# The last product of a decoder layer: four PSUM tiles, groups of two, one and one, and a half row in two pieces

## The chip, the cores and the metric

The kernel runs on one core of one Trainium2 chip. The core has TensorE (PE in the profile, its weight loads PEld), VectorE (DVE), ScalarE (ACT), GpSimd (POOL) and SyncE (SP, which here only starts transfers). Tiles live in SBUF; matmuls write into PSUM, which has banks of 512 f32 columns on each of 128 partitions. The metric is the device time of one execution in microseconds, as the median of several runs. The profile is one execution more, with a time of its own.

## The reference

One layer of a hybrid decoder on 1024 tokens of width 1024, in float32: a combined input projection, four heads of differential attention and four of mLSTM, an output projection with a residual, and a gated MLP (width 2816, with a causal convolution of width 3) with a residual and a final RMSNorm. What matters here are the last lines:

```python
    hn = rmsnorm(x, ffn_norm_w[l])
    u = causal_dwconv(hn @ w_up[l], ffn_conv_w[l], ffn_conv_b[l])
    gate, up = jnp.split(u, 2, axis=-1)
    x = x + (jax.nn.silu(gate) * up) @ w_down[l]
return rmsnorm(x, final_norm_w)
```

where `rmsnorm(x, w)` is `x * rsqrt(mean(x*x) + 1e-6) * w`, taken over a token's row of 1024.

## The kernel before

A product in float32 is made of three matmuls of a split operand (high and low part, `mm3b`, lines 162 to 165). The down projection, 1024 x 2816 by 2816 x 1024, is done by a fast scheme of seven products in place of eight: `PORDER = (1, 2, 7, 5, 6, 4, 3)`. Each product has 11 steps along the inner dimension (`NP`), and in each step four token tiles of 128 rows (`tt` from 0 to 3) get three matmuls of 128x512 each, 12 per step. The sums are gathered in eight rows of tiles `x2[0..7]` (128 tokens x 1024), each of which already holds the residual. `x2[4..7]` are complete one product before the end; `x2[0..3]` get their last half row (columns 512 to 1024) from the last product, number 3.

`banks(n)` gives product n its four PSUM regions: for an even n two tiles `big` of 1024 columns (two banks each, two token tiles in each), for an odd n four tiles of 512 columns, two of the tag `mm` and one each of `sa` and `sb`. The products before it, those of the up projection, take `mm`, `big` and the small ones in turn; the last of them writes an `mm` tile, and its result is added on DVE in line 1030.

`dprep_to` prepares the operands of coming steps (splits in line 115 on ACT and 116 on DVE), four steps ahead. `evac` puts the additions of a finished token tile into the list `later`, `work(n)` issues n of them; an addition is line 1202 on DVE (`add`), which reads PSUM and SBUF.

The final RMSNorm is spread out. `half` (line 1227) squares half a row on ACT and sums it through the accumulator, in two instructions; `half1` does it for the half row that is complete earlier, and multiplies it with the norm's weights `fin`. `finish(tts, h)` does the rest for the token tiles `tts`: it turns the sum of the first half into `v` (line 1242), squares the second half, adds its sum (line 1245), takes the reciprocal root on DVE (for several tiles `rsqrt`, lines 75 to 81, and line 1250; for one tile `newton`, lines 878 to 882), scales one half row on ACT (line 1254) and the other on DVE (line 1255), and starts the transfer to `out` from SP's queue (line 1260; for tile 3 in two halves, from ACT's and SP's queues, lines 1257 and 1258).

The last product keeps back its last five steps (`TAIL = 5`): after step 6 they are done token tile by token tile, 15 matmuls each, in the groups of `LAST`:

```python
LAST = ([0, 1, 2], [3])
```

After each group come its additions and its `finish`. The order of instructions on each engine is not written out: a planner orders them by the place in the code and by when it holds them ready, and an instruction of a later line may be put ahead of one that waits. Waits between engines are put in by the same framework.

Of the kernel before, what the change touches and what calls it, by code (L numbers as in the profile page):

```python
# [10 lines left out]
F32 = mybir.dt.float32  # L11
F32R = mybir.dt.float32r
I32 = mybir.dt.int32
AF = mybir.ActivationFunctionType
ALU = mybir.AluOpType
PSUM = bass.MemoryType.PSUM

P = 128
S = 1024
D = 1024  # L20
NT = S // P
# [8 lines left out]
SLOPE = [2.0 ** (-8.0 * (h + 1) / H) for h in range(H)]  # L30
LEAD = 5
DLEAD = 4
LAST = ([0, 1, 2], [3])
HELD = 4
YB = 3
RSC = -2.0 ** -13
# [3 lines left out]
def tile_hybrid(ctx: ExitStack, tc: tile.TileContext, I: dict, out: bass.AP):  # L40
    nc = tc.nc
    V = nc.vector
    A = nc.scalar
# [3 lines left out]
    cp = ctx.enter_context(tc.tile_pool(name="cp", bufs=1))  # L47
# [21 lines left out]
    def sm8(n=8, name="s8"):  # L69
        return sp.tile([P, n], F32, name=name, tag=name)  # L70

    def rsqrt(v, n, k=""):

        y = sm8(n, "rs_a" + k)
        V.tensor_scalar(y.bitcast(I32), v.bitcast(I32), -0.5, 1597463007.0, op0=ALU.mult, op1=ALU.add)
        for i in range(3):
            u = sm8(n, "rs_u" + k)
            V.tensor_tensor(u, y, y, op=ALU.mult)
            V.scalar_tensor_tensor(u, u, -0.5, v, op0=ALU.mult, op1=ALU.mult)
            y2 = sm8(n, f"rs_{i}" + k)  # L80
            V.scalar_tensor_tensor(y2, u, 1.5, y, op0=ALU.add, op1=ALU.mult)
            y = y2
        return y
# [28 lines left out]
    def split(dst, src, loeng, scale=None):  # L112

        if scale is None:
            A.activation(dst[:, 0, :], src, AF.Copy)  # L115
            loeng.tensor_tensor(dst[:, 1, :], src, dst[:, 0, :].bitcast(F32), op=ALU.subtract)  # L116
        else:
            A.activation(dst[:, 0, :], src, AF.Copy, scale=scale)
            V.scalar_tensor_tensor(dst[:, 1, :], src, scale, dst[:, 0, :].bitcast(F32), op0=ALU.mult, op1=ALU.subtract)
# [55 lines left out]
    def small(shape):  # L175

        flip[0] ^= 1
        return psA.t(shape, tag="sa" if flip[0] else "sb")

    def big(shape):  # L180
        return psA.t(shape, tag="big", bufs=2)

    def mmps():
        return psA.t([P, 512], tag="mm", bufs=2)

    def rotate(n):
        return (mmps, lambda: big([P, 512]), lambda: small([P, 512]))[n % 3]()

    def banks(n):
        if n % 2 == 0:  # L190
            b = [big([P, S]) for _ in range(2)]
            return [b[k // 2][:, HV[k % 2]] for k in range(4)]
        return [mmps(), mmps(), small([P, 512]), small([P, 512])]
# [6 lines left out]
    def load_x(i, hf, between=None):  # L200
        f = pa.t(XS, tag="ta", bufs=4)
        for c in ([slice(0, 1), slice(1, 2)] if between else [slice(0, 2)]):
            nc.sync.dma_start(f[:, c, :], I["xT"][:, 2 * i + c.start:2 * i + c.stop, HV[hf]])
            if between and c.start == 0:
                between()
        return f
# [45 lines left out]
    f = load_x(0, 0, lambda: next(g0))  # L252
    next(g0)
    split_x(0, 0, f)
    f = load_x(1, 0)
# [5 lines left out]
    f = load_x(2, 0)  # L261
# [3 lines left out]
    f = load_x(3, 0)  # L265
# [5 lines left out]
    for i in range(4):  # L271
        f = load_x(i, 1)
# [115 lines left out]
    for ct in range(4, 8):  # L388
        for hf in range(2):
            ps = rotate(2 * ct + hf)  # L390
# [406 lines left out]
    x2 = []  # L797
# [78 lines left out]
    def newton(v):  # L876
        y = sm8(1, "rx_0")
        V.tensor_scalar(y.bitcast(I32), v.bitcast(I32), -0.5, 1597463007.0, op0=ALU.mult, op1=ALU.add)
        for i, c in enumerate((3.0, 12.0, 768.0)):
            u, y2 = sm8(1, "rx_u"), sm8(1, f"rx_{i + 1}")  # L880
            V.scalar_tensor_tensor(u, y, v, y, op0=ALU.mult, op1=ALU.mult)
            V.scalar_tensor_tensor(y2, u, -c, y, op0=ALU.add, op1=ALU.mult)
            y = y2
        return y
# [239 lines left out]
    def weights(p, i):  # L1124
        if i % 2 == 0:
            wload(p, i)
        return wb.pop((p, i))
# [28 lines left out]
    def dprep_to(n):  # L1156
        while dp_[0] < min(n, len(steps)):
            p, i = steps[dp_[0]]
            if p in SUMS:
                dst, x_, y, op = SUMS[p]  # L1160
                V.tensor_tensor(blk[dst, i], blk[x_, i], blk[y, i], op=op)
            last = p == PORDER[-1] and i >= NP - 2
            if last and not ext:
                e = pd.t([P, 8, 512], F32R, "a21")
                ext.extend(e[:, 2 * m:2 * m + 2, :] for m in range(4))
            at = (lambda: w2.pop(0) if w2 else pd.t([P, 2, 512], F32R, "w2", 2)) if dp_[0] % 5 == 4 else wtile
            dops[dp_[0]] = [ext.pop(0) if last else at() for _ in range(2)]
            for dst, src in zip(dops[dp_[0]], (blk[OPS[p][0], i], weights(p, i))):
                split(dst, src, V)
            dp_[0] += 1  # L1170

    pd = None
# [15 lines left out]
    pd = Scope("pd")  # L1188
# [3 lines left out]
    x2 = [pd.t([P, D], tag="x2", bufs=8) for _ in range(NT)]  # L1192
    fin = pd.t([P, D], tag="fin")
    acc = {(p, tt): pd.t([P, 512], tag=f"acc{p}", bufs=4) for p in (1, 7) for tt in range(4)}

    def dmm(ps, k, tt, first, last):
        s_, m_ = dops[k]
        t = slice(tt * P, (tt + 1) * P)
        mm3b(ps, s_[:, 0, t], s_[:, 1, t], m_, first, last)

    def add(dst, x, y=None):
        V.tensor_tensor(dst, dst if y is None else x, x if y is None else y, op=ALU.add)  # L1202

    later = []

    def work(n):

        for _ in range(min(n, len(later))):
            later.pop(0)()

    def evac(p, tt, ps):

        h0, h1 = HV
        c11, c12, c21, c22 = x2[tt][:, h0], x2[tt][:, h1], x2[tt + 4][:, h0], x2[tt + 4][:, h1]
        if p in (1, 7):
            A.activation(acc[p, tt], ps, AF.Copy)
        if p == 6:
            a1, a7 = acc[1, tt], acc[7, tt]
            pairs = [(a1, ps), (a7, a1), (c22, a7), (c21, a7), (c12, a1)]
        else:  # L1220
            pairs = [(dst, ps) for dst in {1: [c11], 2: [c11], 5: [c12, c22], 4: [c21], 3: [c12]}.get(p, ())]
        later.extend(lambda d=d, x=x: add(d, x) for d, x in pairs)

    def half(tt, h, part):

        j = pd.t([P, 512], tag="junk")
        A.activation(j, x2[tt][:, HV[h]], AF.Square, accum_out=part)

    part1, part2 = cp.tile([P, NT], F32, name="part1"), cp.tile([P, NT], F32, name="part2")

    def half1(tt, h):

# [1 line left out]
        xx = x2[tt][:, HV[h]]  # L1234
        V.tensor_tensor(xx, xx, fin[:, HV[h]], op=ALU.mult)

    def finish(tts, h):

        n = len(tts)
        c = slice(tts[0], tts[0] + n)  # L1240
        v = sm8(n, f"vx{n}")
        V.tensor_scalar(v, part1[:, c], 1.0 / D, EPS, op0=ALU.mult, op1=ALU.add)
        for tt in tts:
            half(tt, h, part2[:, tt:tt + 1])
        V.scalar_tensor_tensor(v, part2[:, c], 1.0 / D, v, op0=ALU.mult, op1=ALU.add)
        if n == 1:
            r = newton(v)
        else:
            r = rsqrt(v, n, "x")
            V.tensor_scalar(r, r, 1.0 / RSC, None, op0=ALU.mult)  # L1250
        a_, b_ = HV[1 - h], HV[h]
        for i, tt in enumerate(tts):
            xx, ri = x2[tt], r[:, i:i + 1]
            A.activation(xx[:, a_], xx[:, a_], AF.Copy, scale=ri)
            V.scalar_tensor_tensor(xx[:, b_], xx[:, b_], ri, fin[:, b_], op0=ALU.mult, op1=ALU.mult)
            if tt == 3:
                A.dma_start(out[tt, :, a_], xx[:, a_])
                nc.sync.dma_start(out[tt, :, b_], xx[:, b_])
            else:
                nc.sync.dma_start(out[tt], xx)  # L1260

    k = 0
    TAIL = 5
    for n, p in enumerate(PORDER):
        ps = banks(n)
        last = n == len(PORDER) - 1
        for i in range(NP - TAIL if last else NP):
            dprep_to(k + 1 + DLEAD)
            fill(k)
            work(3)  # L1270
            for tt in range(4):
                dmm(ps[tt], k, tt, i == 0, i == NP - 1)
            k += 1
        if not last:
            for tt in range(4):
                evac(p, tt, ps[tt])
            if p == 2:
                later.extend(lambda tt=tt: half1(tt, 0) for tt in range(4))
            elif p == 6:
                later.extend(lambda tt=tt: half1(tt, 1) for tt in range(4, NT))  # L1280
            elif p == 4:
                later.append(lambda: finish(range(4, NT), 0))
        else:
            dprep_to(len(steps))
            for tts in LAST:
                for tt in tts:
                    for i in range(TAIL):
                        dmm(ps[tt], k + i, tt, False, i == TAIL - 1)
                    evac(p, tt, ps[tt])
                work(len(later))  # L1290
                finish(tts, 1)
    psA.close()
    pd.close()
    wp.close()
# [63 lines left out]
```

## Time and profile before

| | |
|---|---|
| median of 3 runs | 1214.32 us (1213.82 to 1214.63) |
| the profiled execution | 1213.26 us, span of its instructions 1211.5 us |
| granted TensorE clock, mean | 0.995 |
| busy: PE, DVE, ACT, POOL | 98%, 74%, 47%, 40% |
| first matmul of the first down product | 991.5 us |
| last matmul | 1201.8 us |
| last instruction that starts a transfer | 1207.7 us |

The span goes from the first instruction to the end of the last; the time of an execution is some 2 us longer. A row of the timeline gives the start, the duration, the engine, the line, the operation, what is written and what is read, and in brackets how long the engine stood idle before it and what ended that. Rows that end in "x2" or "x3" merge neighbours: start of the first, end of the last less that start.

### The profile page before, as it was taken

What the parts mean: (1) busy time and instruction counts of PE and PEld (TensorE: products, weight loads), DVE (VectorE), ACT (ScalarE), POOL (GpSimd) and SP (SyncE); (2) the same over time, 40 slices, a digit from 0 to 9 for tenths busy, and PEclk for the clock granted to TensorE, in tenths of its full rate; (3) what the DMA queues carried; (4) which work ended last, traced back from release to release, by engine and by line L of the source; (5) the groups of instructions that cost most, each with busy time, mean ns of one, the idle gap of its engine ahead of it and who ended that gap; (6) DMA issues with size and microseconds to landing.
All of it is one profiled execution on the core that took longest, in us unless ns stands there. A gap on an engine that the chain in (4) does not pass through costs nothing.

```text
span 1211.5 us, 15939 instructions
## 1 busy us (share of the span) xinstructions
PE 1183.0 (98%) x5622; PEld 973.3 (80%) x5622; DVE 899.2 (74%) x1564; ACT 571.0 (47%) x1114; POOL 480.1 (40%) x364
## 2 busy tenths in 40 slices
PE   9998999999999999999999999999999999999996
PEld 7885788888778878888888888888888888888885
DVE  5598232566767777669998998788887878886694
ACT  6534323334666666344644444434344345544462
POOL 0475451003543431001198887888887600000000
PEclk9998999999999999999999999999999999999999
DMA  8755664124212243332322312222222169823223
GB/s 307 252 206 205 226 243 166 62 71 157 79 52 54 70 157 114 121 127 99 124 70 87 103 72 100 91 70 87 77 80 104 54 217 346 296 96 96 96 79 139
DMA packets 61743, 159.03 MB, mean 131 GB/s; under 512 B 6176, under 2 KB 10464, under 8 KB 61664
## 3 DMA queue, kind: packets, MB, share of 16 engines
q1 hardware_dynamic: 61232, 157.21, 38.0%
q8 instruction: 44, 0.72, 0.3%
q10 hardware_dynamic: 432, 0.82, 0.2%
q14 instruction: 35, 0.29, 0.1%
HBM read 116.02 MB, written 37.78 MB: 127 GB/s over the span
## 4 chain that ended last, share of the span: by engine, by line
PE 84%; DVE 5%; DMA 3%; ACT 3%; POOL 3%; issue 1%; SPq 1%; POOLq 0%; ACTq 0%; DVEq 0%
PE mm L160 6%; PE mm L158 6%; PE mm L159 6%; PE mm L163 5%; PE mm L164 5%; PE mm L165 5%; PE big L158 4%; PE big L160 4%; PE big L159 4%; PE big L164 4%; PE big L165 4%; PE big L163 4%; PE sb L777 3%; POOL vda L327 3%; PE sb L158 2%; PE sb L160 2%
## 5 line engine op out<-in xcount | busy, mean ns | idle before, releaser
L115 ACT ACTIVATE w<-wf 128x512 fp32r<-128x512 f32 x160 | 97.7, 624 | 142.3 <-POOL wf L999 33.6
L116 DVE TENSOR_TENSOR w<-wf,w 128x512 fp32r<-128x512 f32 x128 | 108.4, 858 | 27.9 <-ACT w L115 21.7
L1041 DVE SCALAR_TENSOR_TENSOR y<-x2b,fcw,y 128x1022 f32<-128x1022 f32 x44 | 91.8, 2125 | 0.0
L1040 DVE SCALAR_TENSOR_TENSOR y<-x2b,fcw,y 128x1023 f32<-128x1023 f32 x44 | 75.7, 1762 | 9.4 <-ACT y L1039 9.4
L116 POOL TENSOR_TENSOR w<-s,w 128x512 fp32r<-128x512 f32 x40 | 69.8, 1746 | 6.2 <-ACT w L115 6.2
L327 POOL TENSOR_TENSOR vda<-vda 128x512 f32<-128x512 f32 x24 | 46.6, 1958 | 63.7 <-DMA vda<-in_w_down_dram 62.9
L116 POOL TENSOR_TENSOR w<-wf,w 128x512 fp32r<-128x512 f32 x32 | 46.9, 1469 | 57.0 <-ACT w L115 47.2
L116 POOL TENSOR_TENSOR w<-wu,w 128x512 fp32r<-128x512 f32 x40 | 66.5, 1662 | 1.8 <-ACT w L115 1.8
L158 PE MATMUL mm<-xb,w 128*128 128x512 f32 x168 | 66.1, 394 | 0.0
L160 PE MATMUL mm<-xb,w 128*128 128x512 f32 x168 | 65.9, 392 | 0.0
L159 PE MATMUL mm<-xb,w 128*128 128x512 f32 x168 | 65.9, 392 | 0.0
L968 POOL TENSOR_TENSOR s<-wu 128x512 f32<-128x512 f32 x20 | 36.5, 1825 | 58.0 <-DMA wu<-in_w_up_dram 58.0
L752 DVE CUSTOM_DVE_ANT_0 s<-big,B 128x128 f32<-128x128 f32 (+7 forms) x64 | 47.6, 755 | 13.7 <-PE big L750 12.3
L1039 ACT ACTIVATE y<-x2b,fcw 128x1024 f32<-128x1024 f32 x44 | 52.3, 1237 | 9.6 <-DVE x2b L1030 8.4
L754 ACT ACTIVATE s<-s,mb 128x128 f32<-128x128 f32 (+7 forms) x64 | 49.3, 772 | 11.2 <-DVE mb L753 10.0
L163 PE MATMUL big<-w 128*128 128x512 f32 x132 | 51.5, 390 | 0.8 <-DVE x L1202 0.8
L164 PE MATMUL big<-w 128*128 128x512 f32 x132 | 51.4, 389 | 0.0
L165 PE MATMUL big<-w 128*128 128x512 f32 x132 | 51.3, 389 | 0.0
L115 ACT ACTIVATE w<-wu 128x512 fp32r<-128x512 f32 x48 | 29.7, 625 | 40.1 <-PE mm L160 10.7
L777 PEld LDWEIGHTS sb<-vda,aT 128*128 128x128 f32 x288 | 36.2, 190 | 15.4 <-ACT aT L774 14.6
L777 PE MATMUL sb<-vda,aT 128*128 128x128 f32 x288 | 44.2, 289 | 3.7 <-ACT aT L774 3.1
L115 ACT ACTIVATE w<-hb 128x512 fp32r<-128x512 f32 x41 | 25.8, 630 | 44.9 <-PE big L165 19.8
(514 smaller groups left out, 3769.8 us busy)
## 6 DMA issues: line engine op xcount, KB each, us to landing
wf<-in_w_up_dram SPq DMA_DIRECT2D x22, 512.0 KB, 4.5
actd<-y SPq DMA_DIRECT2D x21, 512.0 KB, 2.6
wu<-in_w_up_dram SPq DMA_DIRECT2D x20, 512.0 KB, 3.4
wf<-in_w_st_dram SPq DMA_DIRECT2D x12, 512.0 KB, 4.2
vda<-in_w_down_dram SPq DMA_DIRECT2D x12, 512.0 KB, 6.6
wsum<-vda SPq DMA_DIRECT2D x12, 512.0 KB, 3.0
wf<-in_w_mv_dram SPq DMA_DIRECT2D x12, 512.0 KB, 5.3
wf<-wsum SPq DMA_DIRECT2D x12, 512.0 KB, 3.4
```

The costliest lines, as they stand in the source:

```text
L115: A.activation(dst[:, 0, :], src, AF.Copy)
L116: loeng.tensor_tensor(dst[:, 1, :], src, dst[:, 0, :].bitcast(F32), op=ALU.subtract)
L158: PE.matmul(ps, sh, mh, start=first, stop=False)
L159: PE.matmul(ps, sh, ml, start=False, stop=False)
L160: PE.matmul(ps, sl, mh, start=False, stop=last)
L163: PE.matmul(ps, sh, w[:, 0, :], start=first, stop=False)
L164: PE.matmul(ps, sl, w[:, 0, :], start=False, stop=False)
L165: PE.matmul(ps, sh, w[:, 1, :], start=False, stop=last)
L327: GP.tensor_tensor(dst, x_, y, op=ALU.subtract)
L777: PE.matmul(ops, aT[:, b * P:(b + 1) * P], vda[k // 2][:, k % 2, h * P:(h + 1) * P], start=k == 0, stop=k == qt)
L1040: V.scalar_tensor_tensor(y[:, 1:], u[:, :S - 1], cw[:, 1:2], y[:, 1:], op0=ALU.mult, op1=ALU.add)
L1041: V.scalar_tensor_tensor(y[:, 2:], u[:, :S - 2], cw[:, 0:1], y[:, 2:], op0=ALU.mult, op1=ALU.add)
```

## The change

The last product gets four PSUM tiles of its own, because `banks` is now called with n + 1, which flips the tags of all seven products: numbers 0, 2, 4 and 6 in order take `mm`, `mm` and the two small ones, numbers 1, 3 and 5 the two `big` ones. The groups become [0, 1], [2] and [3]. `finish` no longer scales: it returns a function `scale` that does, which is called at once for [0, 1] and for the earlier rows. For [2] it is kept, and called within `finish` of [3], behind the square of the first piece. For tile 3 the last half row is added and squared in two pieces of 256 columns (`QS`), each with an accumulator of its own (`part1` and `part2` have one more column for that) and a sum of its own on DVE. The numbers of matmuls, scalings and transfers stay as they were; one addition, one square with its accumulator read, and one small sum on DVE are added in all.

```diff
-LAST = ([0, 1, 2], [3])
+LAST = ([0, 1], [2], [3])
...
-    part1, part2 = cp.tile([P, NT], F32, name="part1"), cp.tile([P, NT], F32, name="part2")
+    part1, part2 = (cp.tile([P, NT + 1], F32, name=f"part{i}") for i in (1, 2))
+    QS = (slice(512, 768), slice(768, 1024))
...
-    def finish(tts, h):
+    def finish(tts, h, between=None):
...
         V.tensor_scalar(v, part1[:, c], 1.0 / D, EPS, op0=ALU.mult, op1=ALU.add)
-        for tt in tts:
-            half(tt, h, part2[:, tt:tt + 1])
-        V.scalar_tensor_tensor(v, part2[:, c], 1.0 / D, v, op0=ALU.mult, op1=ALU.add)
+        if tts[0] == 3:
+            for i, q in enumerate(QS):
+                j = pd.t([P, 512], tag="junk")
+                pt = part2[:, 3 + 5 * i:4 + 5 * i]
+                A.activation(j[:, 0:256], x2[3][:, q], AF.Square, accum_out=pt)
+                if i == 0:
+                    between()
+                V.scalar_tensor_tensor(v, pt, 1.0 / D, v, op0=ALU.mult, op1=ALU.add)
+        else:
+            for tt in tts:
+                half(tt, h, part2[:, tt:tt + 1])
+            V.scalar_tensor_tensor(v, part2[:, c], 1.0 / D, v, op0=ALU.mult, op1=ALU.add)
...
-        for i, tt in enumerate(tts):
-            xx, ri = x2[tt], r[:, i:i + 1]
-            A.activation(xx[:, a_], xx[:, a_], AF.Copy, scale=ri)
...
+        def scale():
+            for i, tt in enumerate(tts):
+                xx, ri = x2[tt], r[:, i:i + 1]
+                A.activation(xx[:, a_], xx[:, a_], AF.Copy, scale=ri)
+                V.scalar_tensor_tensor(xx[:, b_], xx[:, b_], ri, fin[:, b_], op0=ALU.mult, op1=ALU.mult)
+                if tt == 3:
+                    A.dma_start(out[tt, :, a_], xx[:, a_])
+                    nc.sync.dma_start(out[tt, :, b_], xx[:, b_])
+                else:
+                    nc.sync.dma_start(out[tt], xx)
+
+        return scale
...
-        ps = banks(n)
+        ps = banks(n + 1)
...
-                later.append(lambda: finish(range(4, NT), 0))
+                later.append(lambda: finish(range(4, NT), 0)())
...
+            scale = None
             for tts in LAST:
                 for tt in tts:
                     for i in range(TAIL):
                         dmm(ps[tt], k + i, tt, False, i == TAIL - 1)
-                    evac(p, tt, ps[tt])
+                    if tt < 3:
+                        evac(p, tt, ps[tt])
+                    else:
+                        for q in QS:
+                            add(x2[3][:, q], ps[3][:, q.start - 512:q.stop - 512])
                 work(len(later))
-                finish(tts, 1)
+                if tts == [2]:
+                    scale = finish(tts, 1)
+                else:
+                    finish(tts, 1, scale)()
```

More of the change, by code (lines that the diff above doesn't have):

```diff
@@ L1251, in finish @@
         a_, b_ = HV[1 - h], HV[h]
-        for i, tt in enumerate(tts):
-            xx, ri = x2[tt], r[:, i:i + 1]
[L1254 to L1260, printed above, removed]
+        def scale():
[9 more added lines that the diff above has]
+        return scale
     k = 0
```

## The prediction

> **What bounds the kernel now.** I read the page's busy shares and the shares of its chain first, then a table of busy time by stretch over the last two hundred microseconds, then the timeline of the last twenty, engine by engine.
>
> ```profile
> span 1211.5 us, 15939 instructions
> PE 1183.0 (98%) x5622; PEld 973.3 (80%) x5622; DVE 899.2 (74%) x1564; ACT 571.0 (47%) x1114; POOL 480.1 (40%) x364
> PE 84%; DVE 5%; DMA 3%; ACT 3%; POOL 3%; issue 1%; SPq 1%; POOLq 0%; ACTq 0%; DVEq 0%
> ...
> 1051.00:1081.00 30.00, 30.00 (x134) 24.86 (x133) 29.77 (x50) 16.28 (x32) 0.00 (x0) 1.00 0.31 102
> 1171.00:1187.00 16.00, 16.00 (x72) 13.24 (x71) 13.59 (x32) 10.98 (x23) 0.00 (x0) 1.00 0.39 148
> ...
> 1187.00:1190.50 3.50, 3.50 (x17) 2.90 (x16) 0.00 (x0) 0.00 (x0) 0.00 (x0) 1.00 0.01 1
> 1197.50:1201.00 3.50, 2.72 (x12) 2.10 (x12) 2.13 (x10) 0.72 (x2) 0.00 (x0) 1.00 0.00 0
> 1204.00:1207.70 3.70, 0.00 (x0) 0.00 (x0) 2.52 (x10) 1.44 (x3) 0.00 (x0) 0.72 0.88 348
> ```
>
> The columns of the lower rows are the stretch, its length, then PE, PEld, DVE, ACT, POOL, granted clock, DMA share and GB/s. In these stretches PE is busy without a gap until 1197; DVE and ACT have nothing to do from 1187; PE loses 0.78 us in 1197.5 to 1201; behind 1202 a chain of DVE and ACT runs alone. So the change can win only in the tail, and only what lies between the last matmuls and the last output transfer. The tail itself:
>
> ```profile
> 1194.34 1.29 DVE L1202 TENSOR_TENSOR x<-x,big 128x512 f32<-128x512 f32 x2 [9.40 <-PE big L165]
> 1195.13 0.63 ACT L1227 ACTIVATE junk<-x 128x512 f32<-128x512 f32 x1 [11.09 <-DVE x L1202]
> 1197.32 0.39 PE L165 MATMUL big<-a 128*128 128x512 f32 x1
> 1197.74 0.69 DVE L1202 TENSOR_TENSOR x<-x,big 128x512 f32<-128x512 f32 x1 [2.11 <-PE big L165]
> 1198.49 0.50 PE L163 MATMUL big<-w 128*128 128x512 f32 x1 [0.78 <-DVE x L1202]
> 1198.53 0.63 ACT L1227 ACTIVATE junk<-x 128x512 f32<-128x512 f32 x1 [1.92 <-DVE x L1202]
> 1198.82 0.40 PE L164 MATMUL big<-w 128*128 128x512 f32 x1
> 1199.28 0.16 DVE L1245 SCALAR_TENSOR_TENSOR vx<-part,vx 128x3 f32<-128x3 f32 x1 [0.85 <-ACT junk L1227]
> 1201.65 1.95 ACT L1254 ACTIVATE x<-x,rs_2x 128x512 f32<-128x512 f32 x3 [2.40 <-DVE rs_2x L1250]
> 1201.65 2.08 DVE L1255 SCALAR_TENSOR_TENSOR x<-x,rs_2x,fin 128x512 f32<-128x512 f32 x3
> 1201.79 0.39 PE L165 MATMUL big<-a 128*128 128x512 f32 x1
> 1203.64 0.68 DVE L1202 TENSOR_TENSOR x<-x,big 128x512 f32<-128x512 f32 x1
> 1204.42 0.63 ACT L1227 ACTIVATE junk<-x 128x512 f32<-128x512 f32 x1 [0.82 <-DVE x L1202]
> 1205.17 0.16 DVE L1245 SCALAR_TENSOR_TENSOR vx<-part,vx 128x1 f32<-128x1 f32 x1 [0.85 <-ACT junk L1227]
> 1206.90 0.75 DVE L1255 SCALAR_TENSOR_TENSOR x<-x,rx,fin 128x512 f32<-128x512 f32 x1
> 1207.68 0.33 SPq L1258 DMA_DIRECT2D out_dram<-x  x1
> ```
>
> Three losses stand here. The matmuls of token tile 3 should have started one slot behind 1197.32 (slots are 0.227 us) but waited for tile 2's addition, which reads the other half of the same PSUM tile. Tile 3's last matmul is done at 1201.79 + 0.39 = 1202.18, but its addition starts at 1203.64, because the three scalings of L1255 stand ahead of it on DVE. From that addition on everything is serial: addition to scaling's end 4.01 us, and 3.85 us more to the end of the span (transfer and what follows).
>
> **Part 1: four PSUM tiles.** Each token tile gets a tile of its own. That the wait goes by whole tile is shown earlier too, at the end of the first product:
>
> ```profile
> 1019.16 0.39 PE L165 MATMUL big<-w 128*128 128x512 f32 x1
> 1019.84 0.39 PE L165 MATMUL big<-w 128*128 128x512 f32 x1
> 1020.26 1.09 ACT L1216 ACTIVATE acc<-big 128x512 f32<-128x512 f32 x2 [0.72 <-PE big L165]
> ```
>
> ACT was idle, token tile 0 was complete at 1019.16 + 0.39 = 1019.55, yet its copy started at 1020.26, behind token tile 1 (1019.84 + 0.39). With own tiles the additions can start 0.42 us after the start of the last matmul (1197.32 to 1197.74): tile 0 at 1190.94, tile 1 at 1194.34, tile 2 at 1197.74, and tile 3, fifteen slots (3.40 us) later, at 1201.14. PE's own gain is 1.07 us (1201.79 + 0.42, less 1201.14).
>
> [...]
>
> The parity of all seven products flips: the first down product, on two-bank tiles before, now takes the `mm` and `sa`/`sb` ones just left by the last up products.
>
> ```profile
> 991.28 0.39 PE L160 MATMUL mm<-B22h,w 128*128 128x512 f32 x1
> 991.71 0.69 DVE L1030 TENSOR_TENSOR x2b<-x2b,mm 128x512 f32<-128x512 f32 x1 [1.31 <-PE mm L160]
> 992.18 0.39 PE L163 MATMUL big<-w 128*128 128x512 f32 x1
> ```
>
> One of the two `mm` tiles is still read until 992.40, while token tile 1 wants it at 992.18. If PE waits: 0.28 us with 0.06 us of signalling, and 0.10 us for the slow restart (1198.49 to 1198.82 is 0.33 us where a slot is 0.227): 0.38 us. If the planner puts the other tiles' matmuls first: nothing. No row decides, and the ends are near each other: I take 0.2 us, lost for good since PE has no later gap to absorb it.
>
> **Part 2: groups of two, one, one.** Tiles 0 and 1 need no tile 2 now. Tile 1's half row: addition 1194.34, square from 1195.12 (hop as at 1195.13) to the sum at 1195.87 (0.75, as 1198.53 to 1199.28), chain of roots 2.37 (1199.28 to 1201.65), scaling from 1198.24. Tile 2's addition arrives at 1197.74 in the middle of that chain. Whether it slips in is a matter of order on DVE; these rows speak for it:
>
> ```profile
> 1177.22 0.16 DVE L81 SCALAR_TENSOR_TENSOR rs_0x<-rs_ux,rs_ax 128x4 f32<-128x4 f32 x1
> 1177.33 0.69 DVE L116 TENSOR_TENSOR w<-a,w 128x512 fp32r<-128x512 f32 x1
> 1177.94 0.16 DVE L78 TENSOR_TENSOR rs_ux<-rs_0x 128x4 f32<-128x4 f32 x1
> ```
>
> A split (L116) of a later step of the same product stands within the chain of roots, and the chain's next link is 0.72 us behind the last instead of 0.20. So: tile 2 added by 1198.45, the two scalings move 0.53 us to 1198.77 and occupy DVE until about 1200.1 (0.66 us each: 2.08 less 0.75, over two). ACT squares tile 2's half from 1198.53; its sum and Newton steps start at 1200.1 and take 1.73 us (1205.17 to 1206.90). At 1201.14 tile 3's addition is ready and slips in; Newton ends near 1202.5.
>
> **Part 3: scaling tile 2 behind the next addition.** Its DVE half (0.66 us occupied) and ACT half (0.62: 1.95 over three, less the overlap) move behind the first piece of tile 3's square; its transfer on SP's queue goes with it. That queue then holds it ahead of the last row's half. It is issued near 1203.3; 512 KB at the 348 GB/s of the stretch behind 1204 need 1.5 us, done well before the last rows go near 1205.6. Nothing waits behind it. If it were 1 us later it would cost about that much.
>
> **Part 4: the last half row in two pieces.**
>
> ```profile
> L918 DVE TENSOR_TENSOR hb<-big,hb 128x256 fp32r<-128x256 f32 x16 | 6.7, 421 | 0.0
> L917 ACT ACTIVATE raw<-big 128x256 f32<-128x256 f32 x16 | 6.1, 378 | 0.0
> ```
>
> Whole: addition 0.68, hop 0.10, square and sum 0.75: 1.53 us. In pieces: addition 0.42, hop 0.10, two squares with their accumulators (0.38 + 0.10 each) 0.96, hop 0.02: 1.50 us, if nothing stands between. So this part alone is worth nothing (I take 0), since ACT is as slow as DVE; it adds a 0.16 us sum on DVE beside ACT's work. If ACT's scaling of tile 2 stands between the squares, it costs 0.62 more.
>
> [...]
>
> **The sum.** Tile 3's addition at 1201.14; second square done 1202.65; DVE is then in tile 2's scaling (1202.5 to 1203.16); last sum and Newton to 1204.89; scaling 0.75, end 1205.64 against 1207.65: 2.0 us gained. Less 0.2 at the first product: 1.8 us. The profiled execution took 1213.26 (span 1211.5), 1.06 below the median of 1214.32; the saving is taken off the median: **1212.5 us**.
>
> **Rivals.** (a) The last row goes first: tile 2's Newton and scaling yield DVE, so the second square is followed at once by the last steps: 1202.65 + 1.73 + 0.75 = 1205.1, 2.5 us gained, with no wait at the first product: 1211.8 us. For it: the parts to yield are short. Against: they come earlier in the code. (b) Everything goes in the order of the code: tile 2's addition behind the scalings at 1199.57, its Newton done at 1202.81, then tile 3's addition, ACT's scaling of tile 2 ahead of the second square, end at 1207.35: 0.3 us gained, less the wait: 1214.2 us. That is also what it looks like when the groups and pieces do not do what they say. Against: the interleaved rows above. (c) Slower: the flip reorders DVE where it has no room, 29.77 of 30 us busy from 1051. If the operands of two steps came late, PE would wait two steps of twelve slots (2.72 us each): 1214.3 + 5.4 - 1.8 = 1217.9 us. It decides from 4.2 us of PE waiting on; against it, DVE's work there is the same, and steps are prepared four ahead.
>
> **Chances.** About 0.2% (2.4 us) is what a measurement of this kernel tells from no change. Forecast 0.55, and mixtures between it and (b) or (b) itself 0.25, all within 0.2%; (a) 0.14; (c) 0.06. Faster 0.17 (case a and the upper edge of the forecast), same 0.77, slower 0.06. The range runs from (a) with half a microsecond of scatter (the runs shown span 0.8) to (b) with the full wait at the first product and the same scatter: 1211.2 to 1214.9.
>
> **What would show it.** Right: no PE idle near 1197; the last matmul near 1201; the addition of tile 3 as two 128x256 within 0.1 us of it; tile 2's inside the chain of roots; last scaling ending about 2 us sooner. At the first product, a PE gap of 0 to 0.4 us near 992. Wrong: DVE additions standing behind L1255, a scaling on ACT between the two squares, a PE gap of microseconds between 992 and 1187, or the last rows' transfer queued behind tile 2's.

## The result, and the profile after

The changed kernel takes 1227.54 us (median of 5 runs, 1224.45 to 1228.82) beside 1214.32 us for the kernel before in the same comparison (1213.28 to 1215.77). The ratio is 1.0106, 95% interval 1.0092 to 1.012: slower, where no measurable change had been forecast. The profiled execution took 1227.55 us, so its numbers stand for the median.

The page of the changed kernel, its span, busy times and shares of the chain:

```profile
span 1225.4 us, 15953 instructions
PE 1198.1 (98%) x5622; PEld 976.0 (80%) x5622; DVE 902.8 (74%) x1575; ACT 572.0 (47%) x1116; POOL 474.4 (39%) x364
PE 84%; DVE 5%; DMA 3%; POOL 3%; ACT 3%; issue 1%; SPq 0%; POOLq 0%; ACTq 0%; DVEq 0%
```

The count of matmuls is the same, but PE is busy 15.1 us longer (1198.1 for 1183.0), at the same 98%. So PE does not wait more: the same matmuls take longer. Where this happens is told by stretches. First the one of before, then the one of after, in the same 100 us of the up projection (length, then PE, PEld, DVE, ACT, POOL with their counts, granted clock, DMA share, GB/s):

```profile
600.00:700.00 100.00, 100.00 (x442) 82.53 (x441) 93.55 (x78) 44.66 (x63) 84.70 (x51) 1.00 0.26 88
```

```profile
600.00:700.00 100.00, 100.00 (x430) 80.54 (x429) 93.41 (x82) 44.75 (x62) 83.07 (x49) 1.00 0.28 94
```

PE is busy throughout in both, the clock is granted in full in both, and yet 430 matmuls fit where 442 did. The view of one line's instructions gives shortest, median and longest duration in ns and first and last start, before and then after:

```profile
L158 PE MATMUL big<-th,w x120: 389/389/389, 591.5 to 985.4; 128*128 128x512 f32 x120
```

```profile
L158 PE MATMUL big<-th,w x120: 393/398/398, 595.1 to 1000.5; 128*128 128x512 f32 x120
```

And the group of the down product's matmuls in after, between 1021 and 1187 us (busy time and mean ns of one):

```profile
L163 PE MATMUL big<-w 128*128 128x512 f32 x108 | 42.0, 389 | 0.0
```

In line 158 the median went from 389 to 398 ns. The down product's matmuls kept their 389. From the first matmul of `big<-th,w` to the first down matmul ("the up projection" from here on, without its first 6 us), before takes 591.5 to 991.5, 400.0 us; after takes 595.1 to 1006.8, 411.7 us. All of this lies ahead of anything the change was about.

The account of the two profiles: the first down matmul starts 15.3 us later (1006.8 for 991.5). Of this 11.7 us are the up projection, 0.8 us the output projection, which also has `th` as its moving operand (from its first to its last matmul of `th` and `mxT` 520.5 to 572.9 for 517.9 to 569.5), 0.2 us lie between the two, and 2.6 us stand before 517.9. Nearly all of these 2.6 us arise in one place: PE's instructions are still 0.1 us ahead of before's at 122 us and 2.2 us behind at 130 us. PE waits there for the tile `gs`, 2.78 us for 2.02, and behind that wait TensorE got its full clock in before (1.00) and not in after (0.83):

```profile
120.00:130.00 10.00, 7.98 (x41) 6.30 (x40) 6.21 (x10) 5.62 (x8) 4.50 (x4) 1.00 0.73 260
```

```profile
120.00:130.00 10.00, 7.22 (x30) 5.56 (x29) 6.61 (x10) 5.01 (x6) 4.93 (x3) 0.83 0.68 245
```

From the first down matmul to the start of the last scaling (the "down part" from here on) the changed kernel takes 214.05 us where before takes 1206.90 less 991.50, 215.40 us: 1.35 us gained. 15.3 less 1.35 is the 13.9 us between the spans.

The tail, from the timeline of the changed kernel:

```profile
1206.41 0.69 DVE L1202 TENSOR_TENSOR x<-x,mm 128x512 f32<-128x512 f32 x1 [6.00 <-PE mm L165]
1209.81 0.69 DVE L1202 TENSOR_TENSOR x<-x,mm 128x512 f32<-128x512 f32 x1 [2.71 <-PE mm L165]
1213.51 0.17 DVE L1260 TENSOR_SCALAR rs_2x<-rs_2x 128x2 f32<-128x2 f32 x1
1213.58 0.68 DVE L1202 TENSOR_TENSOR x<-x,sb 128x512 f32<-128x512 f32 x1
1214.18 1.41 DVE L1267 SCALAR_TENSOR_TENSOR x<-x,rs_2x,fin 128x512 f32<-128x512 f32 x2
1216.18 0.39 PE L165 MATMUL sa<-a 128*128 128x512 f32 x1
1217.23 0.16 DVE L882 SCALAR_TENSOR_TENSOR rx<-rx_u,rx 128x1 f32<-128x1 f32 x1
1217.31 0.74 DVE L1202 TENSOR_TENSOR x<-x,sa 128x256 f32<-128x256 f32 x2
1217.42 0.72 ACT L1266 ACTIVATE x<-x,rx 128x512 f32<-128x512 f32 x1 [1.76 <-DVE rx L882]
1217.97 0.75 DVE L1267 SCALAR_TENSOR_TENSOR x<-x,rx,fin 128x512 f32<-128x512 f32 x1
1218.05 0.40 ACT L1248 ACTIVATE junk<-x 128x256 f32<-128x256 f32 x1
1218.58 0.42 ACT L1248 ACTIVATE junk<-x 128x256 f32<-128x256 f32 x1
1219.12 0.16 DVE L1251 SCALAR_TENSOR_TENSOR vx<-part,vx 128x1 f32<-128x1 f32 x1 [0.34 <-ACT junk L1248]
1220.85 0.75 DVE L1267 SCALAR_TENSOR_TENSOR x<-x,rx,fin 128x512 f32<-128x512 f32 x1
```

Each tile's addition follows its own last matmul, tile 2's stands with the end of the chain of roots and ahead of the scalings, and the two pieces are there. What went another way: tile 3's last matmul is done at 1216.18 + 0.42, 1216.60, but the first piece is added at 1217.31, behind the last Newton step of tile 2 (1217.23); and ACT's scaling of tile 2 (1217.42) stands ahead of the first square.

### The profile page after: what moved, and what is told of

Read it like the earlier page. It is cut to its first block, busy times and chain, and to the rows that moved or that the text cites. A ratio compares the mean times of both kernels' runs of the same rounds, so it can differ in the third digit from the quotient of the medians.

```text
span 1225.4 us, 15953 instructions
## 1 busy us (share of the span) xinstructions
PE 1198.1 (98%) x5622; PEld 976.0 (80%) x5622; DVE 902.8 (74%) x1575; ACT 572.0 (47%) x1116; POOL 474.4 (39%) x364
## 4 chain that ended last, share of the span: by engine, by line
PE 84%; DVE 5%; DMA 3%; POOL 3%; ACT 3%; issue 1%; SPq 0%; POOLq 0%; ACTq 0%; DVEq 0%
PE mm L158 6%; PE mm L160 6%; PE mm L159 6%; PE mm L163 5%; PE mm L164 5%; PE mm L165 5%; PE big L158 5%; PE big L160 5%; PE big L159 5%; PE big L163 3%; PE big L165 3%; PE big L164 3%; PE sb L777 3%; POOL vda L327 3%; PE sb L158 2%; PE sb L159 2%
## 5 line engine op out<-in xcount | busy, mean ns | idle before, releaser
L116 DVE TENSOR_TENSOR w<-wf,w 128x512 fp32r<-128x512 f32 x128 | 105.0, 832 | 25.8 <-ACT w L115 21.6
L1040 DVE SCALAR_TENSOR_TENSOR y<-x2b,fcw,y 128x1023 f32<-128x1023 f32 x44 | 79.0, 1835 | 10.6 <-ACT y L1039 10.6
L968 POOL TENSOR_TENSOR s<-wu 128x512 f32<-128x512 f32 x20 | 33.9, 1696 | 58.4 <-DMA wu<-in_w_up_dram 58.4
L115 ACT ACTIVATE w<-s 128x512 fp32r<-128x512 f32 x43 | 27.0, 629 | 49.1 <-PE mm L160 17.6
L1030 DVE TENSOR_TENSOR x2b<-x2b,mm 128x512 f32<-128x512 f32 x51 | 34.1, 680 | 19.3 <-PE mm L160 18.5
L1030 DVE TENSOR_TENSOR x2b<-x2b,big 128x512 f32<-128x512 f32 x53 | 35.4, 680 | 17.5 <-PE big L160 16.8
L158 PE MATMUL big<-th,w 128*128 128x512 f32 x120 | 47.6, 397 | 0.0
```

The lines of the kernel that those rows point to most:

```text
L158: PE.matmul(ps, sh, mh, start=first, stop=False)
L1040: V.scalar_tensor_tensor(y[:, 1:], u[:, :S - 1], cw[:, 1:2], y[:, 1:], op0=ALU.mult, op1=ALU.add)
```

## The experiments

The instructions ahead of the down projection are the same in both kernels, and in the same order on each engine. What is not the same is where things lie in SBUF. `part1` and `part2` have nine columns of four bytes in place of eight; the framework places tiles in units of 32 bytes, so that each takes 64 bytes for 32. Every tile that is allocated behind them on the left side of SBUF lies 64 bytes higher per partition: `w`, the weights, at 32480 and steps of 4096 for 32416. The right side, which grows down from the end, stays: `th` at 147360 and steps of 4096, `B22h` at 180128. (Addresses are those in the built programs.) Where the stationary operand (`w`, the weights that PE loads) lies on the left and the moving operand (such as `th`, which streams through) on the right, the distance between them was a multiple of 256 bytes before, and is 192 above one after. By the **theory** the time hangs on the addresses; at first it said that the relative place counted modulo 128 bytes. The **rivals**: the changed instructions themselves or their place in memory, or the absolute address of the left side. In the expectations A is the theory of the addresses, A2 its second form, and B the changed instructions or their place.

**The shift alone.** The kernel before, with 64 unused bytes behind `part2`:

```diff
     part1, part2 = cp.tile([P, NT], F32, name="part1"), cp.tile([P, NT], F32, name="part2")
+    cp.tile([P, 16], F32, name="fill")
```

> The kernel before, with an unused tile of 64 bytes per partition behind part2: every tile of the left side of SBUF from there on lies 64 bytes higher, as in the changed kernel; the instructions are those of before. Theory A (the changed kernel lost its time because the left side moved by 64 bytes against the right side, where th, hb, raw and B22 lie): the first down product starts near 1007 us instead of 991.5, its tail is that of before, so 1229 us (1227.5 plus the 1.4 us that the new tail saves). Rival B (the changed instructions themselves, or where their code lies): 1214.3 us.

Its line of matmuls, and from its timeline the first down matmul:

```profile
L158 PE MATMUL big<-th,w x120: 393/398/398, 595.8 to 1001.2; 128*128 128x512 f32 x120
```

```profile
1007.54 0.40 PE L163 MATMUL big<-w 128*128 128x512 f32 x1
```

The up projection takes 411.7 us, as in the changed kernel; the time is 1229.78 us beside 1216.83, ratio 1.0103 (1.0081 to 1.0124). The down part stays at 215.42. Sixty-four bytes that nothing reads or writes make the whole loss, with before's instructions.

**Two ways to a distance of 128.** The changed kernel with the same unused tile (left side 128 bytes higher than before), and the changed kernel with the pad at the end of the right side twice as large (right side 64 lower):

```diff
+    cp.tile([P, 16], F32, name="fill")
```

```diff
-    ....tile([P, 16], F32, name="padr")
+    ....tile([P, 32], F32, name="padr")
```

> The changed kernel, with the same unused tile of 64 bytes: the left side lies 128 bytes higher than before, so the offset between left and right is again the old one modulo 128. Theory A: the up projection runs at the old rate, and what is left is the new tail: 1214.3 less 1.4 = 1213.0 us (1212.4 to 1213.6). Rival B, and rival C (any move of the left side costs, whatever its size): 1227.5 us.

> The changed kernel, with the pad at the right end 128 bytes instead of 64: the right side moves 64 bytes down, the left side stays 64 bytes higher than before. Both sides are then at 96 modulo 128 where before both were at 32. Theory A (only the offset between the two sides counts): 1213.0 us. Rival D (the left side must lie at 32 modulo 128, whatever the right side does): 1227.5 us. Rival B: 1227.5 us.

The line of matmuls, in the one and in the other:

```profile
L158 PE MATMUL big<-th,w x120: 387/393/404, 596.4 to 998.3; 128*128 128x512 f32 x120
```

```profile
L158 PE MATMUL big<-th,w x120: 387/393/404, 592.7 to 994.5; 128*128 128x512 f32 x120
```

Both take 408.1 us for the up projection (first down matmul at 1004.53 and 1000.79), and 1.0066 (1.005 to 1.0082) and 1.0061 (1.0045 to 1.0077) of the time of before. That moving one side up and the other down gives the same is what a relative place asks for. But 400 was due by modulo 128, so this form of the theory fell.

**Half the shift.** The kernel before with 32 bytes (`[P, 8]`), distance 224:

> The kernel before, with the left side 32 bytes higher (at 64 modulo 128), the right side in place. Theory A with a grain of 64 bytes gives either no loss (1214.3 us) or the whole one (1229 us), with a grain of 32 bytes a loss of its own in between; rivals B 1214.3 us. Theory A alone does not say which; the run is to find the grain.

```profile
L158 PE MATMUL big<-th,w x120: 392/396/397, 594.2 to 999.3; 128*128 128x512 f32 x120
```

The up projection takes 411.4 us (first down matmul at 1005.64), and the run 1.0089 (1.0072 to 1.0105) of the time of before. So the grain is finer than 64 bytes, and the theory now reads: multiples of 256 bytes between the two operands are free, other distances cost, in an amount that has to be measured.

**Back to a multiple of 256, in two ways.** The changed kernel without the pad, so that the right side moves up by 64 like the left; and the changed kernel with eight columns, the second accumulator of the last row put in a column of another tile:

```diff
-    ctx.enter_context(tc.tile_pool(name="pad", bufs=1, side="right")).tile([P, 16], F32, name="padr")
```

```diff
-    part1, part2 = (cp.tile([P, NT + 1], F32, name=f"part{i}") for i in (1, 2))
+    part1, part2 = (cp.tile([P, NT], F32, name=f"part{i}") for i in (1, 2))
...
-                pt = part2[:, 3 + 5 * i:4 + 5 * i]
+                pt = (part2[:, 3:4], ssx[:, 0:1])[i]
```

> The changed kernel without the 64-byte pad at the right end: left and right side both lie 64 bytes higher than before, so the distance from the weights w to the moving operands on the right (th, hb, raw, B22) is that of before, 256 modulo 4096 bytes; in e1 it was 192, in e2 and e3 128, in e4 224, and all four were slow in the up projection. Theory A2 (the distance from the stationary to the moving operand sets the rate, and a multiple of 256 is free): up projection 400.0 us as before, first to last of the down part 1.3 us less: ratio 0.9989. Rival E (any other address than the tuned one is slow, on either side): up projection 408 to 412 us, ratio 1.006 to 1.010.

> The changed kernel with part1 and part2 at their old 8 columns; the second piece's sum goes to a column of ssx, a tile that is no longer in use there. Every address is that of before. All theories of addresses: up projection 400.0 us, the down part 1.3 us less than before, ratio 0.9989 (0.998 to 1.000). Rival B (the instructions of the tail, or where code lies): ratio 1.010.

Without the pad (one line less, so L157), then with eight columns:

```profile
L157 PE MATMUL big<-th,w x120: 389/389/389, 594.6 to 988.4; 128*128 128x512 f32 x120
```

```profile
L158 PE MATMUL big<-th,w x120: 389/389/389, 596.0 to 989.9; 128*128 128x512 f32 x120
```

Both have 389 ns and 400.0 us back (first down matmul at 994.55 and 995.98). They take 0.9995 (0.9982 to 1.0008) and 0.9989 (0.9981 to 0.9998) of the time of before. The first has every address of the slow kernel on the left, and every instruction of it: the absolute address of the left side and the instructions are out as causes. Both have a down part of 214.05 us, as the changed kernel has.

**The cost by itself.** A kernel with nothing but matmuls of fp32r, 128x512, each with its own weight load, 60 per distance; the layer is not computed, the output is filled with a loaded tile:

```python
for i in range(60):
    k = i % 4
    PE.matmul(ps, W[:, k * P:k * P + P], M[:, o // 4:o // 4 + 512], start=i == 0, stop=i == 59)
```

> Not the layer: only 17 runs of 60 matmuls of 128x512 in fp32r, each with its own weight load (four weight slices of 512 bytes in turn), nothing else running beside; the output is filled with a loaded tile. The run oa has the moving operand at a multiple of 4096 bytes from the weights, the next ones 32, 64, 96, 128, 160, 192, 224, 256, 320, 384, 448, 512, 768, 1024 and 2048 bytes further. Theory A2: 0.2267 us from matmul to matmul at 0, 256, 512, 768, 1024 and 2048, and more in between: 0.2331 at 64 and 192, 0.2312 at 128, 0.2330 at 224 (the up projections' 411.7, 408.1 and 411.4 us over 400.0). Rival F (it is the traffic of the other engines, which the addresses only bring into step): the same 0.2267 everywhere.

The timeline has one row for each distance (`oa` 0, `ob` 32, `oc` 64, `od` 96, `oe` 128, `of` 160, `og` 192, `oh` 224, `oi` 256, `oj` 320, `ok` 384, `om` 512, `on` 768):

```profile
22.77 13.76 PE L60 MATMUL oa<-M,W 128*128 128x512 f32 x60
36.37 14.17 PE L60 MATMUL ob<-M,W 128*128 128x512 f32 x60
50.37 13.91 PE L60 MATMUL oc<-M,W 128*128 128x512 f32 x60
64.11 14.17 PE L60 MATMUL od<-M,W 128*128 128x512 f32 x60
78.12 14.16 PE L60 MATMUL oe<-M,W 128*128 128x512 f32 x60
92.12 14.21 PE L60 MATMUL of<-M,W 128*128 128x512 f32 x60
106.17 14.16 PE L60 MATMUL og<-M,W 128*128 128x512 f32 x60
120.18 14.16 PE L60 MATMUL oh<-M,W 128*128 128x512 f32 x60
134.17 13.79 PE L60 MATMUL oi<-M,W 128*128 128x512 f32 x60
147.80 13.91 PE L60 MATMUL oj<-M,W 128*128 128x512 f32 x60
161.55 14.11 PE L60 MATMUL ok<-M,W 128*128 128x512 f32 x60
...
189.50 13.78 PE L60 MATMUL om<-M,W 128*128 128x512 f32 x60
203.12 13.76 PE L60 MATMUL on<-M,W 128*128 128x512 f32 x60
```

A matmul's pace is the distance between the starts of two rows over 60. It is 0.2267 us at 0 (36.37 less 22.77), 0.2335 at 192 (120.18 less 106.17), 0.2332 at 224, 0.2272 at 256 (147.80 less 134.17) and 0.2270 at 512. In the kernel, 0.2267 times 411.7 over 400.0 is 0.2333 at 192, and the same sum gives 0.2332 at 224: the bench has it with the other engines all but idle (a DVE copy of 0.16 us for each distance). At 64 the bench gives 0.2290 (64.11 less 50.37), where 0.2331 had been expected from the kernel at 192. At 128 the bench says 0.2333 and the kernel 0.2313 (408.1 us).

The traces show where kernel and bench part. In 170 of 582 steps of three matmuls the moving operand's low part is `x2a`, which lies on the left as `w` does. The two moved together, so their distance stayed a multiple of 256, and by the theory these matmuls of line 159 should have kept the 389/389/389 that they have in before. In the changed kernel, and then in the one with the unused tile (distance 128), they have:

```profile
L159 PE MATMUL big<-x2a,w x56: 389/398/400, 595.3 to 999.3; 128*128 128x512 f32 x56
```

```profile
L159 PE MATMUL big<-x2a,w x56: 388/388/396, 596.7 to 997.1; 128*128 128x512 f32 x56
```

Steps with `hb`, whose moving operands all lie on the right, keep nearly the bench's pace in the kernel, as means from start to start: 0.2333 us a matmul at 192, 0.2333 at 224 and 0.2321 at 128. Steps with `x2a` have 0.2334, 0.2331 and, at 128, only 0.2291. So the distance between a matmul's own two operands does not settle its pace alone. The operands of the matmuls just before and after it are the obvious candidate; no run separates them.

**The pad taken from the kernel before.** The same line removed as above; distance 320, on the other side:

> The kernel before without the pad at the right end: right side 64 bytes higher, left in place, so the distance from weights to moving operand is 320 modulo 4096 where it was 256. Theory A2 with the measured pace of the offset 320 (13.75 us per 60 matmuls against 13.60): the up projection takes 400.0 x 13.75 / 13.60 = 404.4 us; first down matmul to the last scaling 215.4 as before. If a move of the right side to 96 modulo 128 is what counts, as much as any other: 408 to 412 us; if only the left side counts: 400.0 us.

```profile
L157 PE MATMUL big<-th,w x120: 388/394/398, 594.1 to 994.0; 128*128 128x512 f32 x120
```

First down matmul at 1000.18: 406.1 us, where 404.4 was worked out from the bench's 0.2292. The direction is right and the size off by 1.7 us. Again it is the steps with `x2a` that leave the bench's pace: 0.2330 us against 0.2289 for those with `hb`. The single run took 1221.99 us. The pad of 64 bytes in the kernel before is thus worth 6.1 us of its up projection.

**The change's own parts.** Free of the shift, the kernel before with only the flip of the tags, so that the last product has four PSUM tiles and the groups stay as they were:

```diff
-        ps = banks(n)
+        ps = banks(n + 1)
```

> The kernel before with banks(n + 1) alone; addresses as before. PE should run through the tail without the 0.78 us wait, so tile 3's addition is no longer behind the three scalings, but ACT still scales three tiles ahead of tile 3's square. By the rows of before and of e6: tile 2's addition 206.4 us behind the first down matmul, scalings 3.9 later at 210.3, square of tile 3 behind three ACT scalings (1.95) at 212.2, sum 212.9, last scaling starts at 214.7 us, against 215.40 before and 214.05 with the whole change. If the flip brought all of the gain: 214.05; if none: 215.4. Up projection 400.0 us.

```profile
1202.38 0.68 DVE L1202 TENSOR_TENSOR x<-x,sa 128x512 f32<-128x512 f32 x1
1202.51 1.95 ACT L1254 ACTIVATE x<-x,rs_2x 128x512 f32<-128x512 f32 x3 [2.40 <-DVE rs_2x L1250]
1204.36 0.61 ACT L1227 ACTIVATE junk<-x 128x512 f32<-128x512 f32 x1
1206.83 0.75 DVE L1255 SCALAR_TENSOR_TENSOR x<-x,rx,fin 128x512 f32<-128x512 f32 x1
```

The first down matmul is at 992.19, so the down part takes 214.64 us, 0.76 less than before. Tile 3's addition no longer stands behind the three scalings; but its square now waits for ACT's three (1202.51 + 1.95), so most of the win is lost again there. The single run took 1213.26 us.

And the change without the split and without the extra column, the scaling of tile 2 still behind tile 3's square. There is a single run of it and a timed one:

```diff
+            half(3, h, part2[:, 3:4])
+            between()
+            V.scalar_tensor_tensor(v, part2[:, c], 1.0 / D, v, op0=ALU.mult, op1=ALU.add)
...
-                    if tt < 3:
-                        evac(p, tt, ps[tt])
-                    else:
-                        for q in QS:
-                            add(x2[3][:, q], ps[3][:, q.start - 512:q.stop - 512])
+                    evac(p, tt, ps[tt])
```

> As e6, with tile 3's last half row added and squared whole. The prediction put the split at nothing. By the rows of the changed kernel ACT's scaling of tile 2 stood ahead of the first piece's square (at 1217.42, square at 1218.05), so a whole addition would have been ready before ACT was free: from the first down matmul to the start of the last scaling 214.05 us with the split, 213.8 without. If the split were worth what it is meant for, the time without it would be longer, 214.3 or more.

> The version without the split and without the shift, timed. Its part behind the first down matmul was 1.63 us shorter than before in the trace (213.77 against 215.40): ratio 1 - 1.63 / 1216.4 = 0.9987, between 0.998 and 0.9995, and 0.3 us below the version with the split.

The tail of the timed one:

```profile
1204.07 0.68 DVE L1202 TENSOR_TENSOR x<-x,sa 128x512 f32<-128x512 f32 x1
1204.18 0.72 ACT L1262 ACTIVATE x<-x,rx 128x512 f32<-128x512 f32 x1 [1.76 <-DVE rx L882]
1204.84 0.63 ACT L1227 ACTIVATE junk<-x 128x512 f32<-128x512 f32 x1
1205.59 0.16 DVE L1247 SCALAR_TENSOR_TENSOR vx<-part,vx 128x1 f32<-128x1 f32 x1 [0.18 <-ACT junk L1227]
1207.32 0.75 DVE L1263 SCALAR_TENSOR_TENSOR x<-x,rx,fin 128x512 f32<-128x512 f32 x1
```

The down part is 213.76 us (first down matmul 993.56; 213.77 in the single run, whose time was 1213.67 us), and the time 1214.44 us beside 1216.65, ratio 0.9985 (0.9975 to 0.9995). This is the best version: some 0.15% faster than before, and by the two ratios 1.2% faster than the change as made (0.9985 over 1.0106). The split then adds 0.29 us (214.05): whole, the addition takes so long that ACT is through with the scaling of tile 2, and the square starts at 1204.84, 0.09 us behind the addition's end; in pieces, the first could be squared at some 1217.83 (1217.31, an addition of 0.42 and a hop of 0.10, estimates of the prediction from rows of before), but ACT comes to it at 1218.05, behind that scaling.

## Why the prediction was wrong

**The step that failed is one that is not there.** The prediction counts additions, squares, sums, waits and queues, and takes its saving off the median: all that lies ahead of the tail stands in the sum as unchanged. The extra column of `part1` and `part2` has no sentence and no term, so its cost was put at nothing without a reason. Through the addresses it cost 11.7 us in the up projection and 0.8 in the output projection, 12.5 us, and 1.35 were gained in the tail. The medians differ by 13.2; the 2 us that remain are of the size of the 2.3 us that the wait for `gs` and the clock behind it took in the profiled execution, and these aren't the change's (see below). None of the signs listed as fatal came: no PE gap, no late addition behind the scalings of [0, 1], no queued transfer.

**The sum in the tail** was right on the four PSUM tiles, wrong on two orders, and too large: 1.8 us forecast and 1.35 measured (215.40 less 214.05).

- PE's own gain: 1.07 less 0.2 forecast. The last matmul stands 209.38 us behind the first down matmul (1216.18 less 1006.80) where it stood 210.29 (1201.79 less 991.50): 0.91 for 0.87. No gap near tile 3 is left, and PE is busy 195.10 of 195.10 us from 1021.4 to 1216.5. The forecast that own tiles end the wait held. DVE's addition of tile 2 from `sb` (1213.58, 0.68 us) runs while PE fills `sa`, and the matmuls' starts stay 0.22 to 0.23 us apart there (1213.46, 1213.69, 1213.92, 1214.14, 1214.37). Whether the two halves of one `big` tile could have been filled and read side by side without the wait of 0.78 us isn't shown: the change takes the shared tile away together with the wait.
- The wait at the first product: 0.2 us taken. The planner let one matmul of `sb` go first:

```profile
1007.50 0.39 PE L163 MATMUL sb<-w 128*128 128x512 f32 x1
1007.75 0.50 PE L163 MATMUL mm<-w 128*128 128x512 f32 x1
1008.08 0.40 PE L164 MATMUL mm<-w 128*128 128x512 f32 x1
```

  The step from 1007.50 to 1008.08 is 0.58 us where two slots are 0.45: some 0.13 us, near enough, between the bounds of 0 and 0.38.
- "At 1201.14 tile 3's addition is ready and slips in" failed. It was ready, and started 0.71 us later (1217.31 for 1216.60), when the last of tile 2's Newton steps was done. That tile 2's addition slips into the chain of roots was also only half so: it stands at its end (1213.58, behind L1260), in time for the scalings. So the planner put both additions at the end of a chain, not at the first free place. For the start of the last addition 2.3 us were forecast (2.50 less 0.2) and 1.63 measured (210.51 us behind the first down matmul, 212.14 before): 0.67 us less.
- From the last addition to the last scaling 3.75 us were forecast against 3.26 before, and 3.54 were measured, so 0.21 of the 0.67 come back. ACT's scaling of tile 2 did not come between the two squares, but ahead of the first.
- Part 4 was taken at nothing; it lost 0.29 us. "If nothing stands between" was the condition, and something stood ahead. From the first square to the sum the pieces take 1.07 us (1218.05 to 1219.12), the whole 0.75 (1204.84 to 1205.59). The head start that was to pay for this is gone, as ACT is late: the first square starts 0.74 us behind the start of the addition in pieces and 0.77 whole.
- Taken alone, the flip gave 0.76 us, groups and deferral another 0.88 (214.64 to 213.76), the split took 0.29 back: 1.35.

**The rivals.** (c) had the sign and not the mechanism: it placed the loss in PE waits behind a reordered DVE, and PE has no wait there. (b), in the order of the code, came by half: tile 2's addition is ahead of the scalings, against it, but tile 3's addition stands behind tile 2's Newton steps and ACT's scaling of tile 2 ahead of the second square, as in (b). So the tail is one of the mixtures of forecast and (b) that had a chance of their own. (a) did not come, since the last row never went first.

**What stays open.** Why the clock between 120 and 130 us differs from execution to execution isn't shown. In the profiles of all twelve runs of the layer it was below 1.00 there where PE had waited 2.31 us or longer for `gs`: in the changed kernel as made, with the unused tile, without the pad and with eight columns, and in the kernel before without the pad. It was 1.00 where PE had waited 2.27 us or less, the kernel before with 64 more bytes among them. So it goes neither with the shift nor with the changed instructions; that the length of the wait is the cause isn't tested. A planner order that starts the last addition 0.71 us sooner wasn't tried. And why a distance off 256 bytes slows the matmul isn't shown, nor how a neighbour's operands come into it: the bench takes away the other engines, but not the weight load that runs beside the matmul (one for each, 187 to 188 ns in the median).

## What to carry to other kernels

Count a change in the size of a small, early allocated tile as a change to the addresses of all that lies behind it, and compare addresses as well as instructions; if matmuls far from the edit get a few nanoseconds longer at the full granted clock (here 389 to 398 ns in the median at 1.00), look there first. Keep the distance from weights to moving operand at a multiple of 256 bytes (on the bench 0.2267 to 0.2272 us a matmul at 0, 256 and 512, and 0.2290 to 0.2342 at 64, 320 and the distances from 128 to 224), and put new accumulators into columns that exist. A split of the last step lost 0.29 us here, where the engine that takes the pieces was still busy when the first one came: look at that engine first.

## What the runs showed of the hardware

The pace of an fp32r matmul of 128x512 with its own weight load depends on how far its two operands lie apart in a partition: 0.2267 to 0.2272 us at 0, 256 and 512 bytes, 0.2290 at 64, 0.2292 at 320, and 0.2332 to 0.2342 at 128, 160, 192 and 224, up to 3.3% more, at a granted clock of 1.0. In this kernel the worst of it is 11.7 us of 400. The down product, whose operands all lie on one side and moved together, kept its 389 ns. That alone is no protection: the matmuls of `x2a` and `w` moved together too, but stand among matmuls with `th`, and their median went from 389 to 398 ns.
